# A two-layer hybrid block in split fp32: the FFN's gate and up products go token-major, and their product is turned on chip and kept whole

## The chip, the cores and the metric

The kernel runs on one core of one Trainium2 chip. The metric is the time of one execution on the device in microseconds (us); of several executions the median is given.

## The reference

Two layers work on 256 tokens of width 2048. Each adds a mixer's output to the residual and then an FFN's. Layer 0's mixer is a gated delta rule beside an RG-LRU, layer 1's two kinds of attention; the change does not touch the inside of either. All arrays are float32. What matters here is the FFN, whose hidden width is 5632:

```python
DEPTH = 2; D_MODEL = 2048; SEQ = 256; D_FF = 5632

def rmsnorm(x, w):
    xf = x.astype(jnp.float32)
    y = xf * lax.rsqrt(jnp.mean(xf * xf, axis=-1, keepdims=True) + NORM_EPS)
    return (y * w.astype(jnp.float32)).astype(x.dtype)

def swiglu(hn, w_gate, w_up, w_down):
    return (jax.nn.silu(hn @ w_gate) * (hn @ w_up)) @ w_down

for layer in range(DEPTH):
    h = h + mixer[layer](rmsnorm(h, ...), ...)
    h = h + swiglu(rmsnorm(h, ffn_norm[layer]),
                   ffn_w_gate[layer], ffn_w_up[layer], ffn_w_down[layer])
return rmsnorm(h, final_norm)
```

## The kernel before

**Split operands.** TensorE multiplies in the type float32r. Every float32 operand is split exactly into two such parts: `hi`, a rounded copy, and `lo`, the float32 value minus `hi`. A product is then three matmuls that accumulate in PSUM: hi by hi, hi by lo and lo by hi. The normalised activations are the tile `X`, held feature-major: 16 feature tiles of 128, each with a hi and a lo row of 256 tokens. `to_x` makes it from the residual `h` (token-major, in SBUF throughout): for each feature tile two transposes on TensorE (L239), an ACT operation that writes hi (L240) and a DVE operation that writes lo (L241). `X` holds h times the norm's weight only; the reciprocal root of the mean square comes in later, on the results (`rstd` makes it as one column for each token half, `rstd_rows` as a row over the tokens).

**Weights** arrive from HBM in units of 128 x 1024 (half a megabyte) on SP's queue. `unit` (L145) takes a unit into a raw tile and splits it in two halves of 512 columns (`HALF`): an ACT copy makes hi (L156), a DVE subtraction lo (L157). Pools give 3 raw, 4 hi and 3 lo buffers, for the whole kernel.

**Two forms of product.** In `wstat` the weights are stationary: a 128x128 weight tile is loaded and the columns of `X` move, so the result is feature-major, [128 features, 256 tokens]. In its wide form the hi weights take hi and lo of `X` together in one matmul of 512 columns (L172; the two products stand side by side in PSUM), and the lo weights take hi of `X` in one of 256 columns (L177). In `xstat` a 128x128 tile of the activations is stationary and 512 weight columns move; the result is token-major, two tiles of [128 tokens, 512 features], with three matmuls (L217, L218, L219) for each k and token half. `out_proj` uses it for the outputs of the mixers and of the FFN, and adds each result to `h` on DVE (L270).

**The FFN** (L283) works in three pieces of 16, 16 and 12 hidden tiles of 128. For each hidden tile it runs a wide `wstat` for gate and one for up. `scaled` adds the two halves of each result and multiplies by the row of `rstd`, ACT takes Silu, GpSimd multiplies gate by up (L302), and ACT and DVE split the product into the tile `gt` (L303, L304). The hidden activations are feature-major, as the down products need them. A piece ends with its down products: `out_proj` over four column groups of 512, with the piece's 8 or 6 units each, which are added to `h`. So `h` is read and written three times an FFN. After the last piece `norm_then` starts the next norm's sums of squares and `to_x` for each group as it is done.

**Order.** The program gives the order of a step's instructions. Background work of the mixers is in generators; `tick`, called after each unit of weights, advances them by a stage. The framework then orders the instructions of each engine and places the semaphores. SBUF pools and two PSUM pools (`acc`, 4 banks for accumulators, and `msp`, 4 banks for transposes and small products) are made once and serve the mixers and the FFNs.

Of the kernel before, what the change touches and what calls it, by code (L numbers as in the profile page):

```python
# [6 lines left out]
ALU = mybir.AluOpType  # L7
# [3 lines left out]
D = 2048          # model width  # L11
T = 256           # tokens
NK = D // 128     # 16 feature tiles
NH = 8            # heads of each mixer half
FF = 5632
NJ = FF // 128    # 44 hidden tiles
# [3 lines left out]
# columns of the packed per-feature array  # L20
# [7 lines left out]
# constant tables (of shapes alone)  # L28
# [7 lines left out]
NTAB0 = 152       # the part that is needed first  # L36
HALF = 512         # columns of a weight unit that are split at a time
HB = 8            # heads whose columns are kept


def body(tc, A, out):
# [8 lines left out]
    ogp = pool("og", 3)  # L50
# [3 lines left out]
    mx = pool("mx", 1)  # L54
    acc = pool("acc", 4, space=PSUM)
    msp = pool("msp", 4, space=PSUM)
# [50 lines left out]
    # background work: generators that are advanced by a stage each time some weights have been used  # L107
# [7 lines left out]
    def step(t):  # L115
        """one stage of a task."""
# [4 lines left out]
    def run(gen):  # L121
        """a generator in one go; what it returns."""
# [22 lines left out]
    def unit(src):  # L145
        """half a megabyte of weights, split exactly into two float32r parts."""
# [7 lines left out]
        for i in range(0, 1024, HALF):  # L154
            s = slice(i, i + HALF)
# [27 lines left out]
    def scaled(P, name, scale=1.0, tag="t1", bufs=5):  # L183
        """the two halves of a wide tile together, times scale and the tokens' rstd."""
# [9 lines left out]
    def xstat(xk, srcs, tail=0):  # L194
        """two token-major output tiles [128 tokens, 512 features]; xk(k): [128, 2, 256] split operand.

        tail: the first tile is through with the last units before the second one takes them.
        """
# [3 lines left out]
        for u, src in enumerate(srcs):  # L202
            w = [t.rearrange("p (k n) -> p k n", n=512) for t in unit(src)]
# [7 lines left out]
            for u1, (hi, lo), tt in todo:  # L211
                for kk in range(2):
                    k = 2 * u1 + kk
                    x = xk(k)
                    for t in tt:
# [3 lines left out]
                        PE.matmul(Ps[t], x[:, 1, ts], hi[:, kk], start=False, stop=k == n - 1)  # L219
            tick()  # L220
        return Ps

# [9 lines left out]
    def to_x(g, w, late=False):  # L232
        """feature-major split operand of h * w for column group g."""
# [19 lines left out]
    def rstd_rows():  # L253
        """rstd of the tokens along the free axis, on every partition."""
# [10 lines left out]
    def out_proj(xk, srcs4, then=None, tail=0):  # L265
        for g in range(4):
            Ps = xstat(xk, srcs4(g), tail if g == 3 else 0)
# [15 lines left out]
    def ffn(L, then, tail=0):  # L283
        gu, dn = A[f"gu{L}"], A[f"dn{L}"]
        j = 0
        for piece in (16, 16, 12):
            tiles = []
            for jj in range(piece):
                if jj % 8 == 0:
                    tiles.append(ogp.tile([128, 8, 2, T], F32R, name="gt", tag="og"))  # L290
                dst = tiles[-1][:, jj % 8]
                Pg = wstat(gu[2 * j], True)
                if j == 0:
                    rstd()
                    Pu = wstat(gu[1], True)
                    rstd_rows()
                a = scaled(Pg, "fa")
                S.activation(a, a, AF.Silu)  # L298
                if j:
                    Pu = wstat(gu[2 * j + 1], True)  # L300
                b = scaled(Pu, "fb")
                G.tensor_tensor(out=b, in0=a, in1=b, op=ALU.mult)  # L302
                S.copy(dst[:, 0], b)  # L303
                V.tensor_sub(dst[:, 1], b, dst[:, 0].bitcast(F32))  # L304
                j += 1
            last = j == NJ
            j0 = (j - piece) // 2
            out_proj(lambda k: tiles[k // 8][:, k % 8], lambda g: [dn[g, j0 + u] for u in range(piece // 2)],
                     then if last else None, tail if last else 0)

# [1 line left out]
    def small_proj(src, n):  # L312
        """token-major [128, 2, n] of rmsnorm(h) @ W for a few columns."""
# [22 lines left out]
    def conv(P, w, bias=None):  # L336
        """causal 4-tap convolution along the tokens of P * rstd."""
# [12 lines left out]
    def mixer0():  # L350
        W = A["w0w"]
# [56 lines left out]
        def lru_scan():  # L408
            # y = -log a; 1 - a^2 = tanh(y) (1 + a^2)
# [43 lines left out]
        def head_task(hd, qk, c):  # L453
            """transposes, norms, decay and the products within the chunks of one head."""
# [24 lines left out]
            # per-token columns [chunk, head]: 0 rq/sqrt(d), 1 beta rk^2, 2 1/rk, 3 beta rk^2 exp(Gtot-G)  # L479
# [22 lines left out]
            CA, Cb = mats[gr][:, 0:2], mats[gr][:, 2]  # matrices m = 4 * chunk + head  # L502
# [13 lines left out]
        def group_task(gr):  # L516
# [5 lines left out]
            # P = inverse of I + C (strictly upper part of C); Xi holds the diagonal 32-blocks of its transpose  # L522
# [16 lines left out]
            # 16-blocks row by row  # L539
# [15 lines left out]
            # 16 -> 32  # L555
# [15 lines left out]
            # 32 -> 64  # L571
# [13 lines left out]
            # chunks  # L585
# [54 lines left out]
            # rms over the head, gate  # L640
# [40 lines left out]
        for hd in range(NH):  # L681
# [14 lines left out]
            for which, wi in ((0, 1), (1, 0), (2, 2)):  # L696
                first = hd == 0 and which == 2  # the rows of rstd come as late as the accumulators allow
# [36 lines left out]
    def mixer1():  # L734
# [4 lines left out]
        def forget():  # L739
# [8 lines left out]
            # minus the running sums of log f along the tokens, a head on each partition  # L748
# [93 lines left out]
    for g in range(4):  # L842
        start(to_x(g, cl["n0"]))
    finish()
    mixer0()
    ffn(0, norm_then(cl["n2"]))
    mixer1()

# [129 lines left out]
```

## Time and profile before

| what | value |
|---|---|
| median of 3 runs | 2336.7 us (2336.26 to 2337.09) |
| span of the profiled execution | 2334.5 us (the page gives no other time of that execution) |
| TensorE matmuls (PE) | 2312.4 us busy, 99%, 13,074 |
| TensorE weight loads (PEld) | 1996.1 us, 86%, 13,074 |
| VectorE (DVE) | 1529.0 us, 65%, 3,166 |
| ScalarE (ACT) | 1211.6 us, 52%, 2,476 |
| GpSimd (POOL) | 120.6 us, 5%, 160 |
| DMA | 420.54 MB, mean 180 GB/s |

A line like L172 is a line of the kernel; `Pw<-X,whi` means that it writes the tile `Pw` and reads `X` and `whi`. `xN` counts instructions, then come their busy time in us and the mean of one in ns. In the time line a row has the start, the length, the engine, the line, the operation, and in brackets the idle time of the engine before it and what ended it. A matmul's record is longer than its share of PE, because matmuls overlap in the pipeline: the rate is read from the distance between starts, or from a stretch of time and its count.

### The profile page before, as it was taken

What the parts mean: (1) busy time and instruction counts of PE and PEld (TensorE: products, weight loads), DVE (VectorE), ACT (ScalarE), POOL (GpSimd) and SP (SyncE); (2) the same over time, 40 slices, a digit from 0 to 9 for tenths busy, and PEclk for the clock granted to TensorE, in tenths of its full rate; (3) what the DMA queues carried; (4) which work ended last, traced back from release to release, by engine and by line L of the source; (5) the groups of instructions that cost most, each with busy time, mean ns of one, the idle gap of its engine ahead of it and who ended that gap; (6) DMA issues with size and microseconds to landing.
All of it is one profiled execution on the core that took longest, in us unless ns stands there. A gap on an engine that the chain in (4) does not pass through costs nothing.

```text
span 2334.5 us, 35623 instructions
## 1 busy us (share of the span) xinstructions
PE 2312.4 (99%) x13074; PEld 1996.1 (86%) x13074; DVE 1529.0 (65%) x3166; ACT 1211.6 (52%) x2476; POOL 120.6 (5%) x160
## 2 busy tenths in 40 slices
PE   8999999999999999999999999999999999999998
PEld 8999888888888888888878888888888888888886
DVE  6899767666655665566656658867665566655665
ACT  7665654555544554455554445545554455544554
POOL 0211200000000000000000000000000000000000
PEclk9999999999999999999999999999999999999999
DMA  6445445555555555655555455555565655555564
GB/s 202 155 152 156 136 145 181 181 189 190 191 193 188 187 189 190 191 188 189 184 172 169 150 169 170 170 187 180 190 191 192 190 189 185 185 198 187 185 206 162
DMA packets 117375, 420.54 MB, mean 180 GB/s; under 512 B 12976, under 2 KB 14512, under 8 KB 117072
## 3 DMA queue, kind: packets, MB, share of 16 engines
q1 hardware_dynamic: 117200, 418.27, 55.5%
q8 instruction: 102, 1.67, 0.3%
q14 instruction: 73, 0.60, 0.1%
HBM read 416.12 MB, written 2.10 MB: 179 GB/s over the span
## 4 chain that ended last, share of the span: by engine, by line
PE 97%; DVE 1%; DMA 1%; ACT 0%; issue 0%; SPq 0%; ACTq 0%; DVEq 0%
PE Pw L172 34%; PE Pw L177 20%; PE Px L217 11%; PE Px L218 11%; PE Px L219 11%; PE Pw L175 2%; PE Pw L176 2%; PE Pt L239 1%; PE Psc L782 0%; DMA raw<-in_w0w 0%; DVE wlo L157 0%; PE Ps L321 0%; PE Pkk L505 0%; DMA h<-in_x 0%; PE Pss L467 0%; PE PoT L809 0%
## 5 line engine op out<-in xcount | busy, mean ns | idle before, releaser
L157 DVE TENSOR_TENSOR wlo<-raw,whi 128x512 fp32r<-128x512 f32 x1568 | 1046.0, 699 | 686.4 <-issue 491.1
L156 ACT CAST whi<-raw 128x512 fp32r<-128x512 f32 x1568 | 922.0, 620 | 805.5 <-PE Px L219 315.1
L172 PE MATMUL Pw<-X,whi 128*128 128x512 f32 x3456 | 1219.4, 398 | 0.0
L177 PE MATMUL Pw<-X,wlo 128*128 128x256 f32 x3968 | 1112.1, 280 | 0.0
L172 PEld LDWEIGHTS Pw<-X,whi 128*128 128x128 f32 x3456 | 648.9, 188 | 157.2 <-issue 0.7
L177 PEld LDWEIGHTS Pw<-X,wlo 128*128 128x128 f32 x3968 | 750.1, 189 | 0.4
L217 PE MATMUL Px<-whi,gt 128*128 128x512 f32 x704 | 274.2, 390 | 0.0
L219 PE MATMUL Px<-whi,gt 128*128 128x512 f32 x704 | 273.9, 389 | 0.0
L218 PE MATMUL Px<-wlo,gt 128*128 128x512 f32 x704 | 273.9, 389 | 0.0
L302 POOL TENSOR_TENSOR fb<-fa,fb 128x256 f32<-128x256 f32 x88 | 65.8, 748 | 1832.9 <-DVE fb L189 1227.0
L217 PEld LDWEIGHTS Px<-whi,gt 128*128 128x128 f32 x704 | 132.2, 188 | 27.6
L219 PEld LDWEIGHTS Px<-whi,gt 128*128 128x128 f32 x704 | 132.2, 188 | 27.3
L218 PEld LDWEIGHTS Px<-wlo,gt 128*128 128x128 f32 x704 | 132.2, 188 | 27.2
L175 PE MATMUL Pw<-X,whi 128*128 128x256 f32 x512 | 149.0, 291 | 0.0
L176 PE MATMUL Pw<-X,whi 128*128 128x256 f32 x512 | 145.3, 284 | 0.0
L303 ACT CAST gt<-fb 128x256 fp32r<-128x256 f32 x88 | 35.9, 407 | 151.7 <-POOL fb L302 151.7
L175 PEld LDWEIGHTS Pw<-X,whi 128*128 128x128 f32 x512 | 98.6, 192 | 0.9 <-ACT whi L156 0.3
L176 PEld LDWEIGHTS Pw<-X,whi 128*128 128x128 f32 x512 | 98.6, 193 | 0.4
L270 DVE TENSOR_TENSOR h<-Px,h 128x512 f32<-128x512 f32 x80 | 54.9, 688 | 36.8 <-PE Px L219 36.8
L217 PE MATMUL Px<-whi,X 128*128 128x512 f32 x192 | 77.2, 402 | 0.0
L218 PE MATMUL Px<-wlo,X 128*128 128x512 f32 x192 | 75.9, 395 | 0.0
L298 ACT ACTIVATE fa<-fa 128x256 f32<-128x256 f32 x88 | 36.8, 418 | 75.4 <-DVE fa L189 75.3
(302 smaller groups left out, 1782.4 us busy)
## 6 DMA issues: line engine op xcount, KB each, us to landing
raw<-in_gu SPq DMA_DIRECT2D x352, 512.0 KB, 3.3
raw<-in_dn SPq DMA_DIRECT2D x176, 512.0 KB, 3.4
raw<-in_w0w SPq DMA_DIRECT2D x80, 512.0 KB, 3.4
raw<-in_wo SPq DMA_DIRECT2D x64, 512.0 KB, 3.4
raw<-in_w1w SPq DMA_DIRECT2D x64, 512.0 KB, 3.4
raw<-in_w1x SPq DMA_DIRECT2D x32, 512.0 KB, 3.4
raw<-in_w0x SPq DMA_DIRECT2D x16, 512.0 KB, 3.3
h<-in_x SPq DMA_DIRECT2D x4, 512.0 KB, 7.4
```

The source lines that it names most:

```text
L156: S.copy(hi[:, s], raw[:, s])
L157: V.tensor_sub(lo[:, s], raw[:, s], hi[:, s].bitcast(F32))
L172: PE.matmul(P.rearrange("p a b -> p (a b)"), hi[:, kk], X[:, k].rearrange("p a b -> p (a b)"), start=k == 0, stop=False)
L175: PE.matmul(P[:, 0], hi[:, kk], X[:, k, 0], start=k == 0, stop=False)
L176: PE.matmul(P[:, 0], hi[:, kk], X[:, k, 1], start=False, stop=False)
L177: PE.matmul(P[:, 0], lo[:, kk], X[:, k, 0], start=False, stop=k == NK - 1)
L217: PE.matmul(Ps[t], x[:, 0, ts], hi[:, kk], start=k == 0, stop=False)
L218: PE.matmul(Ps[t], x[:, 0, ts], lo[:, kk], start=False, stop=False)
L219: PE.matmul(Ps[t], x[:, 1, ts], hi[:, kk], start=False, stop=k == n - 1)
L270: V.tensor_tensor(out=hs, in0=Ps[t], in1=hs, op=ALU.add)
L298: S.activation(a, a, AF.Silu)
L302: G.tensor_tensor(out=b, in0=a, in1=b, op=ALU.mult)
```

## The change

The weights of gate and up are laid out like those of the down products, in units of 256 rows and 512 columns, gate and up side by side. The FFN now makes its hidden activations in 11 blocks of 512 columns (`NB`). A block has 8 steps `u`, each with one unit of gate and one of up; the tiles of `X` are stationary and 512 weight columns move, into four accumulators (two token halves, gate and up). The result is token-major, so the scale of `rstd` is a column: ACT takes Silu with it, and one DVE operation scales up and multiplies. That product is turned by `turn`: four transposes on TensorE into one bank, an ACT copy for hi and a DVE subtraction for lo, both 512 columns, into `hid`, which holds all 44 hidden tiles. The turns of a block are issued after steps 2 and 3 of the next block, the last block's within the first down group. Then one pass of down products over 22 units a group follows, so `h` is added to once an FFN.

`unit` gets a parameter `step`; the FFN's units are split whole, in one ACT copy and one DVE subtraction of 1024 columns. The pools of the mixers (`og`, `mx`) and both PSUM pools are now made anew for each phase (mixer, FFN, mixer, FFN): 4 accumulator and 4 small banks in a mixer, 6 and 2 in an FFN. GpSimd has no work in the FFN any more, and `rstd_rows` is not called there.

```diff
-    ogp = pool("og", 3)
     wr = pool("wr", 3)
     wh = pool("wh", 4)
     wl = pool("wl", 3)
-    mx = pool("mx", 1)
-    acc = pool("acc", 4, space=PSUM)
-    msp = pool("msp", 4, space=PSUM)
+    mx, acc, msp, ogp = Phase(), Phase(), Phase(), Phase()
+
+    def phase(mixer):
+        st = ExitStack()
+        sub = lambda name, bufs, **kw: st.enter_context(tc.tile_pool(name=name, bufs=bufs, **kw))
+        ogp.pool = sub("og", 3) if mixer else sub("hid", 1)
+        mx.pool = sub("mx" if mixer else "fx", 1)
+        acc.pool = sub("acc", 4 if mixer else 6, space=PSUM)
+        msp.pool = sub("msp", 4 if mixer else 2, space=PSUM)
+        return st
...
-    def unit(src):
+    def unit(src, step=HALF):
...
-        for i in range(0, 1024, HALF):
-            s = slice(i, i + HALF)
+        for i in range(0, 1024, step):
+            s = slice(i, i + step)
             S.copy(hi[:, s], raw[:, s])
             V.tensor_sub(lo[:, s], raw[:, s], hi[:, s].bitcast(F32))
...
-    def xstat(xk, srcs, tail=0):
+    def xstat(xk, srcs, tail=0, step=HALF, each=None):
...
-            w = [t.rearrange("p (k n) -> p k n", n=512) for t in unit(src)]
+            w = [t.rearrange("p (k n) -> p k n", n=512) for t in unit(src, step)]
...
+            if each:
+                each(u)
             tick()
...
     def ffn(L, then, tail=0):
         gu, dn = A[f"gu{L}"], A[f"dn{L}"]
-        j = 0
-        for piece in (16, 16, 12):
...
+        hid = ogp.tile([128, NJ, 2, T], F32R, name="hid")
+
+        def turn(b, t, a):
+            P = ms([128, 4, 128], "Ph")
+            for i in range(4):
+                PE.transpose(P[:, i], a[:, i * 128:(i + 1) * 128], tb["ident"])
+            d = hid[:, 4 * b:4 * b + 4, :, t * 128:(t + 1) * 128]
+            S.copy(d[:, :, 0], P)
+            V.tensor_tensor(out=d[:, :, 1], in0=P, in1=d[:, :, 0].bitcast(F32), op=ALU.subtract)
+
+        todo = []
+        for b in range(NB):
+            Ps = [[acc.tile([128, 512], F32, name=f"P{n}{t}", tag="acc") for n in "gu"] for t in range(2)]
+            for u in range(8):
+                w = [[t.rearrange("p (k n) -> p k n", n=512) for t in unit(gu[b, u, i], 1024)] for i in range(2)]
+                for t in range(2):
+                    ts = slice(t * 128, (t + 1) * 128)
+                    for kk in range(2):
+                        k = 2 * u + kk
+                        for i in range(2):
+                            PE.matmul(Ps[t][i], X[:, k, 0, ts], w[i][0][:, kk], start=k == 0, stop=False)
+                            PE.matmul(Ps[t][i], X[:, k, 0, ts], w[i][1][:, kk], start=False, stop=False)
+                        for i in range(2):
+                            PE.matmul(Ps[t][i], X[:, k, 1, ts], w[i][0][:, kk], start=False, stop=k == NK - 1)
+                if u in (2, 3) and todo:
+                    turn(*todo.pop(0))
+                if b == 0 and u == 4:
+                    rstd()
+                tick()
+            for t in range(2):
+                a = mx.tile([128, 512], F32, name="fa", tag="fa", bufs=4)
+                S.activation(a, Ps[t][0], AF.Silu, scale=nrm["rs"][:, t:t + 1])
+                V.scalar_tensor_tensor(out=a, in0=Ps[t][1], scalar=nrm["rs"][:, t:t + 1], in1=a,
+                                       op0=ALU.mult, op1=ALU.mult)
+                todo.append((b, t, a))
+
+        def more(u):
+            if u in (3, 4) and todo:
+                turn(*todo.pop(0))
+
+        out_proj(lambda k: hid[:, k], lambda g: [dn[g, u] for u in range(NJ // 2)], then, tail, 1024, more)
...
-    mixer0()
-    ffn(0, norm_then(cl["n2"]))
-    mixer1()
+        mixer0()
+    with phase(False):
+        ffn(0, norm_then(cl["n2"]))
+    with phase(True):
+        mixer1()
...
-    ffn(1, last, 3)
+    with phase(False):
+        ffn(1, last, 3)
...
-        gt, ut = (wtiles(w, [128 * j for j in range(NJ)]) for w in (gw, uw))
-        r[f"gu{L}"] = ca(np.stack([gt, ut], 1).reshape(2 * NJ, 2, 128, 1024))
+        r[f"gu{L}"] = ca(np.stack([xgroups(w, [512 * b for b in range(NB)]) for w in (gw, uw)], 2))
```

More of the change, by code (lines that the diff above doesn't have):

```diff
@@ L16 @@
 NJ = FF // 128
+NB = FF // 512
 EPS = 1e-6
@@ L38, with tile @@
 HB = 8
+class Phase:
+    def tile(self, *a, **k):
+        return self.pool.tile(*a, **k)
 def body(tc, A, out):
@@ L263, in rstd_rows, with out_proj @@
         nrm["rb"] = rb
-    def out_proj(xk, srcs4, then=None, tail=0):
+    def out_proj(xk, srcs4, then=None, tail=0, step=HALF, each=None):
         for g in range(4):
-            Ps = xstat(xk, srcs4(g), tail if g == 3 else 0)
+            Ps = xstat(xk, srcs4(g), tail if g == 3 else 0, step, each)
             for t in range(2):
@@ L284, in ffn @@
         gu, dn = A[f"gu{L}"], A[f"dn{L}"]
-        j = 0
-        for piece in (16, 16, 12):
[L287 to L293, printed above, removed]
-                    rstd()
[L295 to L309, printed above, removed]
+        hid = ogp.tile([128, NJ, 2, T], F32R, name="hid")
@@ new lines, in turn @@
+        def turn(b, t, a):
[22 more added lines that the diff above has]
+                if b == 0 and u == 4:
+                    rstd()
+                tick()
+            for t in range(2):
+                a = mx.tile([128, 512], F32, name="fa", tag="fa", bufs=4)
+                S.activation(a, Ps[t][0], AF.Silu, scale=nrm["rs"][:, t:t + 1])
+                V.scalar_tensor_tensor(out=a, in0=Ps[t][1], scalar=nrm["rs"][:, t:t + 1], in1=a, op0=ALU.mult, op1=ALU.mult)
+                todo.append((b, t, a))
@@ L840, in mixer1 @@
         out_proj(lambda k: Om[:, k], lambda g: [wo[g, 4 + u] for u in range(4)], norm_then(cl["n3"]))
-    for g in range(4):
-        start(to_x(g, cl["n0"]))
-    finish()
-    mixer0()
-    ffn(0, norm_then(cl["n2"]))
-    mixer1()
+    with phase(True):
+        for g in range(4):
+            start(to_x(g, cl["n0"]))
+        finish()
+        mixer0()
+    with phase(False):
+        ffn(0, norm_then(cl["n2"]))
+    with phase(True):
+        mixer1()
     fin = []
```

## The prediction

> **What bounds the kernel now.** I read the page first, then the sums by stretches of time, then single rows of the time line. The page names TensorE: it is busy for 99% of the span and the chain of waits is 97% PE.
>
> ```profile
> span 2334.5 us, 35623 instructions
> PE 2312.4 (99%) x13074; PEld 1996.1 (86%) x13074; DVE 1529.0 (65%) x3166; ACT 1211.6 (52%) x2476; POOL 120.6 (5%) x160
> PE 97%; DVE 1%; DMA 1%; ACT 0%; issue 0%; SPq 0%; ACTq 0%; DVEq 0%
> ```
>
> A busy PE need not be PE at its peak, so I read rates from stages that do one thing. These stretches are the FFN's stages: the three gate/up pieces of layer 0, one piece of down products, and the three gate/up pieces of layer 1. The columns are the bounds, the length, then busy us and instructions of each engine.
>
> ```profile
> core 0: us, PE busy (x) PEld busy (x) DVE busy (x) ACT busy (x) POOL busy (x), PEclk, DMA share, GB/s
> 452.14:631.07 178.93, 178.93 (x1038) 156.50 (x1037) 118.27 (x226) 96.79 (x200) 11.69 (x15) 1.00 0.58 188
> 631.07:718.13 87.06, 87.06 (x386) 72.09 (x385) 46.98 (x74) 37.14 (x66) 0.74 (x1) 1.00 0.60 194
> 718.13:899.02 180.89, 180.89 (x1025) 156.96 (x1024) 113.60 (x207) 92.80 (x190) 11.05 (x15) 1.00 0.57 186
> 986.12:1121.80 135.68, 135.68 (x770) 117.72 (x769) 85.06 (x155) 69.46 (x142) 8.10 (x11) 1.00 0.58 187
> 1590.38:1769.31 178.93, 178.93 (x1037) 156.44 (x1036) 118.87 (x226) 96.78 (x200) 11.43 (x15) 1.00 0.59 188
> 1856.38:2037.27 180.89, 180.89 (x1026) 156.94 (x1025) 113.60 (x207) 92.81 (x190) 11.05 (x15) 1.00 0.57 186
> 2124.37:2260.04 135.67, 135.67 (x769) 117.69 (x768) 85.08 (x155) 69.45 (x142) 8.11 (x11) 1.00 0.58 186
> ```
>
> PE never pauses in any of them, at full granted clock (1.00), while DVE, ACT and the DMA engines are far from full. So nothing saved on DVE, ACT or POOL shortens the kernel. Only fewer or shorter PE instructions do, and any new wait of PE is paid in full. The six gate/up pieces sum to 990.99 us.
>
> **Gate and up, products.** Before, one feature tile of one k takes a 512-column matmul and a 256-column one: 512 such pairs in 180.89 us are 353 ns a pair. A block of 512 hidden features needs 128 pairs (8 tiles, 16 k). After, it needs 2 token halves x 16 k x 6 = 192 matmuls, all with 512 columns moving and a token tile of X stationary. The columns streamed are the same (98,304); 64 instructions go. The new form is the form of the down products: 384 matmuls in 87.06 us, 226.7 ns each. 22 blocks x 192 x 226.7 ns = 957.6 us, **33.4 us less**.
>
> **Transposes.** The product is now token-major and is turned on PE: two groups of four 128x128 transposes for a block, 44 groups. The nearest row is the mixer's group of three (L803) between matmuls:
>
> ```profile
> 1349.50 0.28 PE L177 MATMUL Pw<-X,wlo 128*128 128x256 f32 x1
> 1349.62 0.49 PE L803 MATMUL PpT<-tab,pr 128*128 128x128 f32 x3
> 1349.84 0.19 PEld L217 LDWEIGHTS Px<-whi,X 128*128 128x128 f32 x1
> 1349.87 0.48 PE L217 MATMUL Px<-whi,X 128*128 128x512 f32 x1
> 1350.18 0.40 PE L218 MATMUL Px<-wlo,X 128*128 128x512 f32 x1
> 1350.42 0.40 PE L219 MATMUL Px<-whi,X 128*128 128x512 f32 x1
> ```
>
> From L177 to L218 pass 0.68 us, where a 256- and a 512-column matmul alone would take 0.12 + 0.23, so three transposes cost 0.33 us, and the spacing right behind them is 0.24 instead of 0.227 for a few matmuls. With a fourth (0.11) and 0.03 for the slow start, a group costs 0.47 us; 44 make **20.7 us more**. Bounds: 0.40 and 0.55 a group, 18 to 24 us. The copies that follow (an ACT and a DVE operation of 512 columns a group) replace more work than they add, and lie beside PE; the down products need their result only near the end of their first group.
>
> **The weight splits are the new wait.** A unit of 1024 columns is now split in one ACT copy (hi) and one DVE subtraction (lo), where before there were two halves of each. Two units, gate and up, are used together, and there are only three lo buffers. Up's lo of one step of u therefore takes the buffer that gate's lo of the step before leaves. In the order of matmuls within a step (24 of them), gate's lo is read last by the twentieth, and up's lo of the next step is first read eight matmuls later. In those 8 x 0.2267 = 1.81 us must fit: the end of that matmul, DVE's start, the whole subtraction, and the weight load that waits for it.
>
> ```profile
> 575.48 0.28 PE L177 MATMUL Pw<-X,wlo 128*128 128x256 f32 x1
> 575.85 1.29 DVE L157 TENSOR_TENSOR wlo<-raw,whi 128x512 fp32r<-128x512 f32 x2 [1.53 <-PE Pw L177]
> 1589.90 0.69 DVE L270 TENSOR_TENSOR h<-Px,h 128x512 f32<-128x512 f32 x1 [0.97 <-PE Px L219]
> 1590.65 0.42 PEld L239 LDWEIGHTS Pt<-tab,h 128*128 128x128 f32 x4 [0.30 <-DVE h L270]
> L304 DVE TENSOR_TENSOR gt<-fb,gt 128x256 fp32r<-128x256 f32 x88 | 37.4, 425 | 1.1 <-ACT gt L303 1.1
> L270 DVE TENSOR_TENSOR h<-Px,h 128x512 f32<-128x512 f32 x80 | 54.9, 688 | 36.8 <-PE Px L219 36.8
> ```
>
> A 512-column matmul ends 0.39 us after its start. DVE follows 0.09 us after the end where a separate wait instruction stands in between (575.76 to 575.85), as it does in the changed order in all but the first step of a block. The subtraction: 425 ns at 256 columns and 688 at 512 give 1.03 ns a column, so 1.21 to 1.23 us at 1024. DVE's end to the weight load is 0.06 us, and a load that could not run ahead costs 0.12 us before its matmul really runs (1349.84: load, then a matmul of 0.48 that started 0.03 later, against 0.39). Sum 1.88 us against 1.81: **PE waits some 0.07 us** a step, and the uneven spacing behind a pause adds 0.02. Of 176 steps, 40 follow a group of transposes, which hides it, and 22 are a block's first, where DVE waits directly and follows 0.04 after the end (as L270 does at 451.66, below), which closes the loop; 114 x 0.09 = **10 us more**. Bounds: 0 (it closes in time), and 30 us (0.22 a step at 136 steps, if the load's whole 0.19 and more is exposed).
>
> The Trainium skill speaks against this edit: "Perfetto Trace Analysis", Optimizing Scalar/DVE Operations, says that where Scalar and Vector aren't full but make bubbles on other engines, smaller instructions let work be done sooner. By that rule halves would close the loop (0.39 + 0.09 + 0.69 + 0.18 = 1.35 us) and this term would be 0; no wait of this kind is in the trace of before.
>
> **The entries of the FFN.** The accumulators now come from new PSUM pools for each phase. In the changed order PE does the last eight transposes of X and its first gate matmul then waits for the last DVE operation on them. Before, PE went straight on with wstat's matmuls (from 452.14) and fitted the transposes in.
>
> ```profile
> 451.23 0.39 PE L219 MATMUL Px<-whi,Od 128*128 128x512 f32 x1
> 451.66 0.69 DVE L270 TENSOR_TENSOR h<-Px,h 128x512 f32<-128x512 f32 x1 [0.97 <-PE Px L219]
> 452.14 0.39 PE L172 MATMUL Pw<-X,whi 128*128 128x512 f32 x1
> 452.87 0.68 DVE L270 TENSOR_TENSOR h<-Px,h 128x512 f32<-128x512 f32 x1
> 454.62 1.54 ACT L240 ACTIVATE X<-Pt,col 128x256 fp32r<-128x256 f32 x4
> 455.23 1.65 DVE L241 SCALAR_TENSOR_TENSOR X<-Pt,col,X 128x256 fp32r<-128x256 f32 x4
> ```
>
> That DVE work ended at 456.88; with 0.18 to the matmul, the entry costs 457.06 - 452.14 = 4.9 us, and a whole-unit subtraction between the two L270 rows adds a little: 5.0. Before's transposes are within the 990.99, so two entries are **10 us more** whole. Bounds: 6 and 14. The end of layer 0's FFN turns X with two PSUM buffers instead of four, and mixer 1 starts behind transposes: **1.5 us more**, 0 to 6.
>
> **Covered, at nothing.** The down products keep their 1056 matmuls a layer; one pass saves only 16 additions to h a layer on DVE, which lies under PE. Their splits are one unit for 12 matmuls (2.72 us), with a buffer free two units ahead. Silu and the product at a block's end use ACT and DVE while two spare PSUM banks take the next block's first half, and both weights of that step are split ahead. If that cover were gone, 22 ends of about 2 us would cost 44 us. SP's queue keeps its units in order; the small loads that now wait for the hidden tile stand where it is just free. Mixer instructions on PE keep their order.
>
> **Sum.** 2334.5 - 33.4 + 20.7 + 10 + 10 + 1.5 = 2343.3 us of span. The runs' median, 2336.7, is 2.2 above the span, and the page tells no other time of that execution, so I add 2.2: 2345.5, said as **2346 us**, +0.4%.
>
> **Rivals.**
> - No change, 2336: the lo parts come in time. Everything hangs on 0.07 us in 1.88, and the durations of the trace are rounded by 0.01 each; then the 10 us go. Against it: that loop has no slack in any row. With entries at their low bound it gives 2328 to 2336.
> - Faster, 2308: four matmuls in a row now have the same stationary tile. A 256-column matmul takes 0.12 us (1349.50 to 1349.62), a 512-column one 0.2267: 256 columns more cost 0.107, and some 0.013 of each matmul doesn't go with its columns. If a repeated tile spares that, four of every six matmuls gain it: 2816 x 0.0134 = 38 us, 2346 - 38 = 2308. It takes over once a repeat spares more than 5 ns. Against it: L217 and L218 share their tile already, each has a load of its own, and their stages run at 226.7.
>
> ```profile
> L217 PEld LDWEIGHTS Px<-whi,gt 128*128 128x128 f32 x704 | 132.2, 188 | 27.6
> L218 PEld LDWEIGHTS Px<-wlo,gt 128*128 128x128 f32 x704 | 132.2, 188 | 27.2
> ```
>
>   The Trainium skill, "TensorE: Matmul & The Clock Gate", Step-by-step: what each phase is for, says loads are separate so that one can serve many matmuls; this trace shows one for each.
> - Slower, 2372: the spacing of 0.23 to 0.24 us seen right after a pause (1350.18 to 1350.42) doesn't settle within 24 matmuls, since each step brings a new pause: 4224 x 0.006 = 26 us.
>
> **How the numbers follow.** Forecast 0.60, no change 0.20, faster 0.05, much slower 0.15. A measurement of this kernel can tell 0.2% (4.7 us) from no change: faster lies below 2332, slower above 2341.4. Range 2331 to 2365: most of the no-change case at its low end (2328 to 2336), above it the upper bounds of the lo wait (+20). Faster 0.10 (0.05 from that rival, 0.05 from the lower part of no change), same 0.17 (the rest of no change, 0.02 of the forecast), slower 0.73.
>
> **What would show it.** Right: gate/up matmuls 226.7 ns apart; PE idle before the matmul with up's lo (released by DVE's lo) 0.05 to 0.1 us some 114 times; transposes 44 x 4, near 0.47 us a group; about 5 us between the last output product of a mixer and the first gate matmul. Wrong: no PE wait on lo, or one over 0.2 us; a spacing away from 227; a PE wait at block ends.

## The result, and the profile after

The changed kernel takes 2350.04 us in the median (4 runs, 2349.57 to 2351.38) against 2336.84 us before: ratio 1.0061, 95% interval 1.0049 to 1.0073. It is slower by 0.6%; the forecast was 2346 in a range of 2331 to 2365. The profiled execution has a span of 2348.1 us, 13.6 more than before.

The page of the changed kernel, the lines that answer to those of before (PE 99% again, with 1240 matmuls and loads fewer; ACT and DVE less busy, and no shorter for it):

```profile
span 2348.1 us, 31468 instructions
PE 2318.6 (99%) x11834; PEld 1939.1 (83%) x11834; DVE 1356.5 (58%) x2250; ACT 1096.4 (47%) x1682; POOL 55.6 (2%) x72
```

The stages, by stretches of time (columns as in the prediction): gate and up of layer 0; down products to the second mixer's first product; that mixer to its last product and 0.23 us; gate and up of layer 1; down products to the end.

```profile
core 0: us, PE busy (x) PEld busy (x) DVE busy (x) ACT busy (x) POOL busy (x), PEclk, DMA share, GB/s
458.61:953.33 494.72, 494.58 (x2192) 400.29 (x2193) 242.95 (x226) 204.08 (x217) 0.00 (x0) 1.00 0.57 185
953.33:1198.87 245.54, 244.68 (x1094) 201.30 (x1092) 121.23 (x116) 105.79 (x123) 0.00 (x0) 1.00 0.59 191
1198.87:1598.64 399.77, 399.77 (x2064) 335.75 (x2063) 271.91 (x625) 193.87 (x424) 0.00 (x0) 1.00 0.52 168
1603.55:2098.83 495.28, 495.28 (x2192) 400.93 (x2193) 242.95 (x226) 204.18 (x217) 0.00 (x0) 0.99 0.57 185
2098.83:2348.10 249.27, 240.44 (x1065) 198.85 (x1063) 120.65 (x120) 102.06 (x113) 2.56 (x2) 0.99 0.58 190
```

Of before, the stages that the prediction does not show: its third piece of down products, the second mixer, and the last piece of down products with the end.

```profile
1121.80:1189.76 67.96, 67.96 (x314) 56.54 (x313) 41.48 (x70) 36.06 (x74) 0.74 (x1) 1.00 0.58 187
1189.76:1590.38 400.62, 400.52 (x2067) 336.31 (x2066) 273.68 (x630) 193.74 (x422) 0.00 (x0) 1.00 0.53 168
2260.04:2334.50 74.46, 65.45 (x290) 53.89 (x288) 42.75 (x77) 34.29 (x68) 3.29 (x3) 0.97 0.55 183
```

So gate and up take 990.0 us, where they took 991.0: all that the longer matmuls save goes again inside the same stage. The down products with what follows them take 494.8 instead of 490.8 (87.06 + 87.10 + 67.96 in layer 0, 87.07 + 87.10 + 74.46 in layer 1), the second mixer 0.9 less. The rest is at the entries: 5.15 us lie between the start of the last output product of a mixer and the first gate matmul, where it was 0.23.

The three costs inside and ahead of gate and up can be read off single rows.

**The lo wait.** The time line of the changed kernel around the start of a step (u = 5 of block 3, both counted from 0; the first row is the step before):

```profile
621.57 0.39 PE L324 MATMUL Pg<-wlo,X 128*128 128x512 f32 x1
622.05 1.23 DVE L172 TENSOR_TENSOR wlo<-raw,whi 128x1024 fp32r<-128x1024 f32 x1 [2.37 <-issue]
623.15 0.39 PE L323 MATMUL Pu<-whi,X 128*128 128x512 f32 x1
623.33 0.19 PEld L324 LDWEIGHTS Pu<-wlo,X 128*128 128x128 f32 x1 [0.21 <-DVE wlo L172]
623.38 0.44 PE L324 MATMUL Pu<-wlo,X 128*128 128x512 f32 x1
623.66 0.39 PE L326 MATMUL Pg<-whi,X 128*128 128x512 f32 x1
```

The last matmul that reads the old lo buffer ends at 621.96, DVE starts 0.09 later, needs 1.23, and the load follows 0.05 after it. The next matmul comes 0.28 us after the one before instead of 0.227. The view of waits has no line for it, since PE itself is never idle; only its loads are. The groups of the page show it, as the idle time ahead of up's lo loads beside that of gate's:

```profile
L324 PEld LDWEIGHTS Pu<-wlo,X 128*128 128x128 f32 x704 | 132.4, 188 | 49.9 <-DVE wlo L172 27.3
L324 PEld LDWEIGHTS Pg<-wlo,X 128*128 128x128 f32 x704 | 132.9, 189 | 26.4
```

**A group of transposes:**

```profile
610.67 0.39 PE L326 MATMUL Pu<-whi,X 128*128 128x512 f32 x1
610.90 0.60 PE L308 MATMUL Ph<-tab,fa 128*128 128x128 f32 x4
611.26 0.48 PE L323 MATMUL Pg<-whi,X 128*128 128x512 f32 x1
611.58 0.39 PE L324 MATMUL Pg<-wlo,X 128*128 128x512 f32 x1
```

From 610.90 to 611.26 are 0.36 us, and the matmul behind them takes 0.32 instead of 0.227: with 0.01 more in the next ones 0.459 us a group.

**The entry of layer 0's FFN**, and the granted clock behind both entries (PEclk):

```profile
453.46 0.39 PE L234 MATMUL Px<-whi,Od 128*128 128x512 f32 x1
453.96 0.66 PE L256 MATMUL Pt<-tab,h 128*128 128x128 f32 x4
455.69 0.66 PE L256 MATMUL Pt<-tab,h 128*128 128x128 f32 x4 [1.08 <-DVE h L287]
456.90 1.65 DVE L258 SCALAR_TENSOR_TENSOR X<-Pt,col,X 128x256 fp32r<-128x256 f32 x4
458.61 0.80 PE L323 MATMUL Pg<-whi,X 128*128 128x512 f32 x1 [2.26 <-DVE X L258]
459.20 0.63 PE L324 MATMUL Pg<-wlo,X 128*128 128x512 f32 x1
459.63 0.63 PE L323 MATMUL Pu<-whi,X 128*128 128x512 f32 x1
...
458.61:461.70 3.09, 3.09 (x7) 2.48 (x8) 1.47 (x10) 0.00 (x0) 0.00 (x0) 0.50 0.00 0
1603.55:1608.40 4.85, 4.85 (x11) 3.80 (x12) 1.47 (x10) 0.00 (x0) 0.00 (x0) 0.50 0.00 0
```

PE waits for the last operation on X, as forecast. What was not forecast: the matmuls behind it are 0.43 us apart, at a granted clock of 0.50, for 3.1 us in layer 0 and some 5 us in layer 1. Against full speed the first steps lose 1.6 and 2.5 us.

### The profile page after: what moved, and what is told of

Same layout as the page of the kernel before. It is cut to its first block, busy times and chain, and to the rows that moved or that the text cites. A ratio compares the mean times of both kernels' runs of the same rounds, so it can differ in the third digit from the quotient of the medians.

```text
span 2348.1 us, 31468 instructions
## 1 busy us (share of the span) xinstructions
PE 2318.6 (99%) x11834; PEld 1939.1 (83%) x11834; DVE 1356.5 (58%) x2250; ACT 1096.4 (47%) x1682; POOL 55.6 (2%) x72
## 4 chain that ended last, share of the span: by engine, by line
PE 97%; DVE 1%; DMA 1%; ACT 0%; issue 0%; SPq 0%; ACTq 0%; DVEq 0%
PE Px L232 11%; PE Px L233 11%; PE Px L234 11%; PE Pu L324 7%; PE Pg L323 7%; PE Pu L323 7%; PE Pu L326 7%; PE Pg L326 7%; PE Pg L324 7%; PE Pw L187 6%; PE Pw L192 6%; PE Pw L190 2%; PE Pw L191 2%; PE Ph L308 1%; PE Psc L815 1%; PE Pt L256 1%
## 5 line engine op out<-in xcount | busy, mean ns | idle before, releaser
L172 DVE TENSOR_TENSOR wlo<-raw,whi 128x512 fp32r<-128x512 f32 (+1 forms) x1040 | 989.6, 965 | 862.2 <-PE Pg L324 300.1
L171 ACT CAST whi<-raw 128x512 fp32r<-128x512 f32 (+1 forms) x1040 | 853.1, 840 | 1105.8 <-PE Pg L326 468.5
L192 PE MATMUL Pw<-X,wlo 128*128 128x256 f32 x1152 | 325.0, 282 | 0.0
L323 PE MATMUL Pg<-whi,X 128*128 128x512 f32 x704 | 279.7, 397 | 4.5 <-DVE X L258 4.5
L324 PE MATMUL Pu<-wlo,X 128*128 128x512 f32 x704 | 281.7, 400 | 0.1
L323 PE MATMUL Pu<-whi,X 128*128 128x512 f32 x704 | 275.6, 391 | 0.0
L326 PE MATMUL Pu<-whi,X 128*128 128x512 f32 x704 | 275.0, 391 | 0.0
L326 PE MATMUL Pg<-whi,X 128*128 128x512 f32 x704 | 274.8, 390 | 0.0
L324 PE MATMUL Pg<-wlo,X 128*128 128x512 f32 x704 | 274.6, 390 | 0.0
L232 PE MATMUL Px<-whi,hid 128*128 128x512 f32 x704 | 274.5, 390 | 0.0
L234 PE MATMUL Px<-whi,hid 128*128 128x512 f32 x704 | 274.2, 390 | 0.0
L187 PE MATMUL Pw<-X,whi 128*128 128x512 f32 x640 | 230.3, 403 | 0.0
L192 PEld LDWEIGHTS Pw<-X,wlo 128*128 128x128 f32 x1152 | 219.6, 191 | 0.3
```

Source lines behind the costliest of these rows:

```text
L171: S.copy(hi[:, s], raw[:, s])
L172: V.tensor_sub(lo[:, s], raw[:, s], hi[:, s].bitcast(F32))
L187: PE.matmul(P.rearrange("p a b -> p (a b)"), hi[:, kk], X[:, k].rearrange("p a b -> p (a b)"), start=k == 0, stop=False)
L192: PE.matmul(P[:, 0], lo[:, kk], X[:, k, 0], start=False, stop=k == NK - 1)
L232: PE.matmul(Ps[t], x[:, 0, ts], hi[:, kk], start=k == 0, stop=False)
L323: PE.matmul(Ps[t][i], X[:, k, 0, ts], w[i][0][:, kk], start=k == 0, stop=False)
```

## The experiments

The length of a step of gate and up (24 matmuls) is the measure below, taken as the distance between the starts of its first matmul and the next step's, in ns, mean of the steps of both layers. At 226.7 ns a matmul it is 5441. Block 0, which holds the entry, and the first step of every block are left out. In brackets is the number of steps; a layer's last step has no next one and is not counted. Times of two traces are best compared from a fixed point, the last output product of the first mixer, since they differ by up to 3.7 us ahead of it (the start-up, below).

| kernel | plain steps | step with a turn at its end (u = 2) | turn before and at its end (u = 3) | turn before it (u = 4) |
|---|---|---|---|---|
| changed | 5522 (78) | 5896 (20) | 5900 (20) | 5543 (20) |
| halves | 5440 | 5798 | 5904 | 5546 |
| order | 5440 | 5797 | 5900 | 5543 |
| noturn | 5515 (98, with u = 2) | | 5523 (40, u = 3 and 4) | |
| best | 5440 | 5798 | 5905 | 5549 |

**Halves.** Only the FFN's gate and up units are split in two operations each again.

```diff
-                w = [[... for t in unit(gu[b, u, i], 1024)] for i in range(2)]
+                w = [[... for t in unit(gu[b, u, i])] for i in range(2)]
```

> Changed kernel, but gate's and up's units are split in two halves of 512 columns again. My theory: every step of a block whose up-lo waits for the whole subtraction (112 steps, 0.08 to 0.10 us each in the trace of the changed kernel) loses that wait, since only half a subtraction stands between the buffer's release and the load: 9 us less, about 2341. Rival 1: the 0.08 us comes from the release of the buffer (three lo buffers for two units a step) and not from the length of the subtraction: then no change, 2350. Rival 2: more and smaller operations on ACT and DVE delay something else: over 2350.

Measured: 2336.4 us (10 runs), ratio to the kernel before 0.9999 (0.9990 to 1.0009), 13.6 us less than the changed kernel where 9 were expected. The same place of the trace, with a subtraction of 512 columns:

```profile
619.54 0.39 PE L323 MATMUL Pu<-whi,X 128*128 128x512 f32 x1
619.54 0.19 PEld L324 LDWEIGHTS Pu<-wlo,X 128*128 128x128 f32 x1
619.77 0.39 PE L324 MATMUL Pu<-wlo,X 128*128 128x512 f32 x1
```

The load is back beside the matmul before it, and every plain step has 5440 ns. Gate and up sum to 978.9 us here against 990.0: 11.1 less, of which some 9.8 is the lo wait, as expected, and 1.2 a shorter stretch of half clock in this execution. Another 1.5 of the 12.5 us between the spans lies ahead of the last product of the first mixer (the start-up, below). The last 1 us between the medians no trace here accounts for.

**Order.** Whole units, but the matmuls of a step in another order.

```diff
-                for t in range(2):
-                    ts = slice(t * 128, (t + 1) * 128)
-                    for kk in range(2):
-                        k = 2 * u + kk
-                        for i in range(2):
+                for i in range(2):
+                    for t in range(2):
+                        ts = slice(t * 128, (t + 1) * 128)
+                        for kk in range(2):
+                            k = 2 * u + kk
...
-                        for i in range(2):
```

> Changed kernel, whole units split as it has them, but the 24 matmuls of a step run gate's twelve first and then up's twelve. Gate's lo buffer is then free 13 matmuls before the step's end and up's next lo is needed 13 matmuls into the next step. My theory: the lo waits go as with halves, 9 us less, about 2341, which says that the loop of release, subtraction and load was the cost and either side of it mends it. Rival: the extra time of a step comes from reading a new lo unit or from alternating four accumulators: then 2350.

Measured: 2337.57 us (10 runs), ratio 1.0007 (0.9998 to 1.0016). The steps are the same 5440 ns, with DVE's operations as long as in the changed kernel. The median is 12.5 us lower, more than the 9 expected; counted from the last output product of the first mixer (449.8 here, 453.5 in the changed kernel), the trace is 9.0 us shorter. Both mends work, so the cost was the loop of release, subtraction and load, and neither the length of the subtraction nor the order alone.

**Banks.** PSUM pools made once. (The small class that hands out the banks in turn is left out here.)

```diff
...
+    accs, swing, msps = pool("acc", 4, space=PSUM), pool("swing", 2, space=PSUM), pool("msp", 2, space=PSUM)
+    def banks(mixer):
+        acc.ring = [accs] * 4 + ([] if mixer else [swing] * 2)
+        msp.ring = [msps] * 2 + ([swing] * 2 if mixer else [])
+        acc.n = msp.n = 0
...
-        acc.pool = sub("acc", 4 if mixer else 6, space=PSUM)
-        msp.pool = sub("msp", 4 if mixer else 2, space=PSUM)
+        banks(mixer)
```

> Changed kernel with PSUM pools made once: four accumulator banks, two small banks and two that serve as accumulators in an FFN and as small banks in a mixer. No new pool at a phase's start, so the first gate matmul of an FFN needn't wait for the last operation on the old banks. My theory: the pause of 5.2 us at each of the two entries shrinks to about 1 to 2 us (transposes still wait for the additions to h), and the half clock after it (1.6 and 2.5 us lost) goes: 9 to 12 us less, 2338 to 2341. Rival: the pause is the data's (X of the last group is needed), so that it stays: 2350.

Measured: 2335.69 us (10 runs), ratio 0.9999 (0.9989 to 1.0008). That is 14.4 us less, more than expected; the profiled execution, the slowest of the ten, has 11.7 us less from the last output product of the first mixer on, within the 9 to 12. Between the last output product and the first gate matmul are 0.23 us at both entries, there is no half clock, and the second mixer follows the down products after 0.23 us, too. The first step is 1.0 us long at each entry; that is no wait for h, but two groups of four transposes that now run between its matmuls, at some 0.5 us each.

**Noturn.** No transposes; the product goes into the hidden tile as it is.

```diff
-            P = ms([128, 4, 128], "Ph")
-            for i in range(4):
-                PE.transpose(P[:, i], a[:, i * 128:(i + 1) * 128], tb["ident"])
+            P = a.rearrange("p (a b) -> p a b", b=128)
```

> Changed kernel without the 176 transposes: the token-major product is split straight from SBUF into the hidden tile, untransposed (this leaves the transposition out). My theory: 44 groups at 0.46 us go (20.2 us), but the 40 steps behind them now show the lo wait of 0.08 us that the groups hid (3.2 us): 17 us less, about 2333. Rival 1: the transposes lie partly in time that PE would wait anyway: less than 10 us gained, over 2340. Rival 2: the groups hid nothing: 20 us less, 2330.

Measured: 2331.05 us (10 runs), ratio 0.9976 (0.9966 to 0.9985). The span is 20.2 us shorter than the changed kernel's, and 3.4 of that lies ahead of the first FFN, so 16.8 are the experiment's: 20.2 of transposes less 3.3 for 40 steps that now show the lo wait (5523 ns against 5441). In the changed kernel the groups hid it. The median alone (19.0 us less, where the theory gave 17 and rival 2 gave 20) could not have told the two apart; the lengths of the steps do. Two costs of a change can cover each other; taking one away gives less than its price.

**Filler.** Eight matmuls whose result nobody reads, in the pause of each entry.

```diff
+                if w is not cl["n2"]:
+                    P = acc.tile([128, 512], F32, name="Pd", tag="acc")
+                    for i in range(8):
+                        PE.matmul(P, X[:, 12, 0, 0:128], X[:, 0].rearrange("p a b -> p (a b)"), start=i == 0, stop=i == 7)
```

> Changed kernel; the pause of PE at each FFN entry stays (it still waits for the last operation on the old banks), but eight matmuls whose result nobody reads run in its last 2.3 us. My theory: the first gate matmuls run at half clock (0.427 us apart) because PE stood idle for 2.3 us before them; with the filler they run at 0.227, and 1.5 to 2.5 us an entry are saved: 3 to 5 us less than the changed kernel. Rival 1: the clock has fallen already in the slack stretch before, when PE waits for the additions to h; then the filler itself runs at 0.427, ends late and nothing is gained, 2350 or 1 to 2 more. Rival 2: the wide spacing comes from something in the first step (new weights, new banks) and not from the clock: then it stays behind the filler.

Measured: 2346.45 us (4 runs), ratio 1.0044 (1.0030 to 1.0057), 3.6 us less than the changed kernel. The trace has the theory at one entry and rival 1 at the other:

```profile
453.43 0.66 PE L256 MATMUL Pt<-tab,h 128*128 128x128 f32 x4 [1.08 <-DVE h L287]
454.55 2.11 PE L300 MATMUL Pd<-X 128*128 128x512 f32 x8 [0.46 <-ACT X L257]
457.05 0.39 PE L328 MATMUL Pg<-wlo,X 128*128 128x512 f32 x1
457.28 0.40 PE L327 MATMUL Pu<-whi,X 128*128 128x512 f32 x1
...
1598.63 3.61 PE L300 MATMUL Pd<-X 128*128 128x512 f32 x8 [0.46 <-ACT X L257]
1602.64 0.40 PE L328 MATMUL Pg<-wlo,X 128*128 128x512 f32 x1
1602.87 0.39 PE L327 MATMUL Pu<-whi,X 128*128 128x512 f32 x1
```

In layer 0 the filler ran at full speed (2.11 us for eight), in layer 1 at half (3.61), after the same pauses of 1.08 and 0.46 us. At both entries the gate and up matmuls behind it were 0.23 us apart from the second on, so the wide spacing belongs to the clock and not to the first step; rival 2 is out. That the median fell by the 3 to 5 us of the theory is in part luck: from the last output product to the end of the first step, layer 0's entry is 1.1 us shorter than in the changed kernel and layer 1's 0.5, and 2.3 of the 3.1 us between the two spans lie ahead of the first FFN. The length of a pause alone does not say whether the clock falls; its place among the clock's windows does (last section).

**Defer.** Pools as in the change, but the last group of X is transposed later.

```diff
-            if g == 3:
+            if g == 3 and w is cl["n2"]:
                 finish()
...
+                if b == 0 and u == 1:
+                    finish()
```

> Changed kernel with its pools made for each phase, but the last group of X is transposed after the second step of the FFN's first block and not before the FFN (its features are used from the seventh step on). PE's first gate matmul then waits only for the additions to h. My theory: the pause falls from 5.2 us to about 2 and the half clock behind it goes: 3 us of pause and 2 of clock an entry, 10 us less, about 2340, the same as with the pools made once; the order is what costs, not the pools as such. Rival: another wait on the old pools takes its place (the small banks at the deferred transposes): 2345 to 2350.

Measured: 2340.2 us (10 runs), ratio 1.0016 (1.0007 to 1.0025). The pauses between last product and first gate matmul are 2.2 us each (450.90 to 453.12 and 1592.83 to 1595.06), and the clock stays up. What is left of the pause is the wait of the new accumulator pool for the additions to h. The medians' 9.8 us agree with the forecast in part by luck: from the last output product of the first mixer on, the trace is 6.4 us shorter, against 11.7 in banks. The shorter pauses give 5.8 and the clock 4.1, but the deferred transposes, which ran in the pause before, now lie between matmuls and take some 1.7 us back, and some kinds of step are up to 0.03 us longer in the mean. So the cost needs both, new pools and transposes ahead of the first gate matmul: order alone takes more than half of it away, and banks that are made once all of it.

**Acc4.** The FFN with 4 and 4 banks, so without spare accumulators at a block's end.

```diff
-        acc.pool = sub("acc", 4 if mixer else 6, space=PSUM)
-        msp.pool = sub("msp", 4 if mixer else 2, space=PSUM)
+        acc.pool = sub("acc", 4, space=PSUM)
+        msp.pool = sub("msp", 4, space=PSUM)
```

> Changed kernel, but with 4 accumulator and 4 small banks in the FFN too (pools still made for each phase). Two things move. At the entry the first gate matmul now waits for the accumulators alone, so the pause shrinks as with the other entry kernels: 8 to 12 us less. At each of the 22 block ends the next block must wait for Silu and the product to free its banks. What the prediction said of that cover (about 2 us an end without it) gives 44 us more, 2382 to 2386 in all. Rival: the first token half of a block is through twelve matmuls before its end and frees its banks in time, so that an end costs 0 to 0.5 us: 2338 to 2350.

Measured: 2338.68 us (10 runs), ratio 1.0011 (1.0002 to 1.0021): the rival. Gate and up take 493.4 and 493.6 us, 1.3 and 1.7 less than in the changed kernel, where the half clock that is gone had cost 1.6 and 2.5, and a block's first step is typically 0.02 us long of 5441, at most 0.17. The two extra banks cover nothing: the first token half of a block is through twelve matmuls (2.7 us) before the end, and its Silu and product are done some 1.3 us before the next block starts (541.58 against 542.86 in one case). The entry is shorter too (2.6 us from last product to first gate matmul, no half clock); that this comes from the same banks lying in the same place as in the mixer is likely, but no run shows it.

**Best.** Order, banks, defer and one line more, which gives the mixers' share of banks back at the down products:

```diff
+        banks(True)
         out_proj(lambda k: hid[:, k], ...)
```

> Changed kernel with three mends together: gate's twelve matmuls of a step before up's twelve, PSUM banks made once and shared (4 and 4 again from the down products on), and the last group of X transposed inside the FFN's first block. My theory: the terms add: no lo wait (9 us), no pause and no half clock at the entries (12 to 14 us), no pause before the second mixer (about 2 us); what is left against the kernel before is 33.4 us fewer for the products and 20 us more for the turns: span about 2322, ratio 0.994 to 0.996 to the kernel before. Rival: the gains don't add, since a mended wait uncovers another (the additions to h at the entry, or raw weights that come late): ratio 0.997 to 1.0.

Measured: 2323.79 us (5 runs, 2323.15 to 2323.94), ratio to the kernel before 0.9946 (0.9934 to 0.9959): it beats both. Gate and up of both layers:

```profile
450.38:939.52 489.14, 489.14 (x2201) 404.96 (x2200) 248.62 (x236) 213.26 (x227) 0.00 (x0) 1.00 0.60 189
1582.74:2071.89 489.15, 489.15 (x2201) 404.96 (x2200) 248.60 (x236) 213.35 (x227) 0.00 (x0) 1.00 0.60 189
```

PE is busy in every us of both, and so it is in the down products of layer 0 and in the second mixer between them. The gains add: what remains of the change is the shorter products (33.5), less the turns (20.2) and the last transposes of X, which now run inside the two first blocks (2.2). That is 11.1 us; from the last output product of the first mixer on, the trace is 11.4 shorter than that of before.

## Why the prediction was right, step by step

| term | forecast, us | measured, us | from |
|---|---|---|---|
| products of gate and up | -33.4 | -33.5 | 24 matmuls in 5440 ns in plain steps of halves, order, best |
| 44 groups of transposes | +20.7 | +20.2 | 0.459 each; noturn |
| lo waits | +10 | +9.8 | 78 x 0.081, 20 x 0.098 (u = 2), 1.5 in block 0 and first steps; halves, order |
| entries, the pause | +10 | +9.8 | 2 x (5.15 - 0.23) |
| entries, half clock | none | +4.1 | 1.6 + 2.5 |
| end of layer 0's FFN, second mixer, end | +1.5 | +1.4 | stages: 3.4 + 0.6 - 0.9, less 1.8 for four turns |
| first mixer | 0 | +1.5 | start-up, below |
| sum of span | +8.8 | +13.3 of 13.6 | |

**What held.** PE bound the kernel in every stage, so ACT's and DVE's savings (115 and 173 us of busy time) gave nothing. The four prices that came from rows of before held to 0.5 us each, by the mechanisms that the prediction names. The fifth, +1.5 for what follows gate and up, is right as a number by luck: the down products of layer 0 with the start of the second mixer cost 2.5, while the second mixer and the end gave 0.9 and 0.3 back, which the prediction had not foreseen. The lo wait was worked out as 0.07 us plus 0.02 out of a sum of 1.88 against a limit of 1.81; it is 0.08. One of its signs did not show: PE was to stand idle before the matmul with up's lo, but only the load waits there, and the cost appears as wider spacing. The count held too: the 40 steps behind a group showed none until the groups went (noturn). The rule of the Trainium skill, "Perfetto Trace Analysis", Optimizing Scalar/DVE Operations, that breaking up operations may let work be done sooner where they cause bubbles on another engine, holds here: halves closes the loop, at 352 operations more on each of ACT and DVE. But order does it as well with the large ones.

**What was mis-sized.** The step "That DVE work ended at 456.88; with 0.18 to the matmul, the entry costs 457.06 - 452.14 = 4.9 us" priced the pause and took the clock behind it for full. Of the 4.8 us between the forecast span (2343.3) and the measured one (2348.1) this is 4.1; the start-up of this one execution is 1.5, and the other terms came out some 1 lower. The fall was no accident of that execution: all eight entries with such a pause (changed, halves, order and noturn) have it, at 1.5 to 2.8 us each. In the medians, 2346 against 2350, the clock alone would be enough to close the gap. The trace of before held the warning: its first mixer has one long wait, and the stretches before and behind it are

```profile
294.83 1.03 PE L583 MATMUL Pi<-gsc,V 32*32 32x32 f32 x16 [4.93 <-DVE gsc L584]
296.38 0.63 PE L219 MATMUL Px<-whi,X 128*128 128x512 f32 x1
296.81 0.63 PE L217 MATMUL Px<-whi,X 128*128 128x512 f32 x1
...
285.00:289.90 4.90, 4.90 (x34) 3.50 (x32) 4.83 (x13) 1.14 (x2) 1.16 (x1) 1.00 0.20 53
294.80:298.00 3.20, 3.17 (x21) 2.74 (x22) 2.55 (x5) 0.00 (x0) 0.00 (x0) 0.50 0.78 279
```

Matmuls 0.43 us apart at a clock of 0.50, behind a pause. The table of stages that I read left the mixers out.

**What was wrong and cost nothing.** "If that cover were gone, 22 ends of about 2 us would cost 44 us": acc4 took the two spare banks away, and the ends cost nothing. The sentence seems to count Silu and product from the block's last matmul; the half that is needed next has its matmuls behind it 2.7 us earlier.

**The rivals.** "No change" hung on the 0.07 us of the lo loop; the loop did not close. "Faster" needed a repeated stationary tile to be cheaper: in a step four of six matmuls repeat it, and they stay 226.7 ns apart, as in the down products. "Slower" needed the spacing not to settle: behind a lo wait it is back at 227 within eight matmuls.

**The start-up.** The last product of the first mixer, whose matmuls the change leaves in their order, starts at 451.9 in the trace of before, 453.5 in that of the changed kernel and at 449.8 to 451.9 in halves, order, noturn, filler, defer and acc4, which have the same mixer. The changed kernel's first products ran slowly for longer:

```profile
16.70 0.41 PE L191 MATMUL Pw<-X,whi 128*128 128x256 f32 x1
18.80 0.28 PE L190 MATMUL Pw<-X,whi 128*128 128x256 f32 x1
```

Matmuls of 256 columns were 0.21 us apart there until 18.0 us, against 0.12 later; in the trace of before the records were down to 0.28 us by 15.65, in that of order by 10.40. (A wait of PE of 1.0 us at 11 to 12 us is in the changed kernel and in order alike, so it is not the difference.) The trace of halves was fast from 9.2 us on, but has another 3.4 us at a clock of 0.50 in the middle of its first mixer. No run varied this. The ten executions of halves lie 4.9 us apart, so it is likely chance from one execution to the next, up to 3.7 us between these traces, and it sets how finely two single profiles of this kernel can be compared; differences are better taken from a fixed point inside them.

## What to carry to other kernels

When PE is busy throughout, price a rewrite by its count of matmuls times the spacing in a stage of the same form, and then look for every place where the new buffers close a loop: release, operation, load, against the matmuls that lie between. A loop that misses by 0.08 us costs that at every turn and shows in no list of PE's waits; look at the loads' idle time and at the spacing. Pools that are made anew at a phase's start turn overlap into a pause, and a pause of PE costs its length and, where it leaves TensorE busy for only about half of 3.4 us or less, in this kernel 1.5 to 2.8 us more at half clock, so keep the banks and let the next phase's first matmuls go ahead of the last transposes.

## What the runs showed of the hardware

- The granted clock of TensorE changes only at bounds that lie 3.41 us apart. From the first rise to full clock to the last fall at the end, every stretch at one clock in the ten traces is a whole number of these long: 3.41 or 6.83 us at 0.50, and for example 157.0, 276.5 or 1140.1 us at 1.00 (46, 81 and 334 of them). Cut along these bounds, the windows read (first four: the changed kernel's entries; last two: the filler's; the third number from the end is the clock):

```profile
454.93:458.34 3.41, 0.66 (x4) 0.42 (x4) 2.55 (x9) 2.81 (x9) 0.00 (x0) 1.00 0.51 161
458.34:461.75 3.41, 3.14 (x7) 2.48 (x8) 1.74 (x11) 0.00 (x0) 0.00 (x0) 0.50 0.00 0
1598.40:1601.81 3.41, 1.71 (x10) 0.84 (x8) 2.55 (x6) 2.87 (x7) 0.00 (x0) 1.00 0.54 190
1601.81:1605.22 3.41, 1.67 (x4) 1.38 (x5) 3.10 (x15) 0.98 (x3) 0.00 (x0) 0.50 0.26 99
451.98:455.39 3.41, 1.87 (x12) 1.27 (x11) 2.55 (x7) 3.30 (x9) 0.00 (x0) 1.00 0.67 231
1595.45:1598.86 3.41, 1.77 (x11) 1.07 (x10) 2.55 (x7) 3.04 (x8) 0.00 (x0) 1.00 0.68 210
```

  A window at full clock in which PE was busy for 0.66 to 1.86 us of 3.41 was followed by half clock at every entry of an FFN, and one with 1.87 us or more by full clock (1.98 and 2.18 in defer). There half clock lasted one window where PE was busy for at least 0.83 of it, and two where it was busy for 0.65 or less of the first. So the two entries of the filler, with the same pauses, differ by where the pauses lie among the windows, as far as these records can tell; in layer 1 of the changed kernel the clock had fallen 1.7 us before the first gate matmul. The limit near 0.55 is as sharp only as these records, and 3.4 us at half clock in the first mixers of halves and banks followed windows full of records, most of them of small matmuls: that stays open. The Trainium skill, "TensorE: Matmul & The Clock Gate", Part 1: The HAM clock gate, puts the fall behind an idle window of some 3.4 us and the return after a busy one, in windows that run freely. The windows and the return agree; the fall came here behind windows in which PE was busy for up to 0.55 of the time, so none was idle.

- A load that waits shows in its matmul as 0.05 us more record (0.44 against 0.39) and in the spacing of the next ones, 0.08 us in all.
